# Seven half products for eight: the expanding products of two feed-forwards as 2x2 block products

## The chip, the core and the metric

The kernel runs on one core of a Trainium2 chip. The metric is the device time of one execution in microseconds (us). The engines named below are TensorE (PE, its weight loads as PEld), VectorE (DVE), ScalarE (ACT), GpSimd (POOL) and the queue of SyncE (SP) that issues the loads of the weights.

## What is computed

Two transformer-like blocks in float32 over 512 tokens of 1024 features, one after the other. Only the two feed-forwards matter here; D_FF is 4096 and D_FF_2 is 2816.

```python
# first block
hf = rmsnorm(x, norm_ff_g)
z = relu(hf @ w_ff1)                      # 1024 -> 4096: the expanding product
x = x + (z * z) @ w_ff2                   # 4096 -> 1024: the contracting product
# second block
h2 = modulate(rms_norm(x, g_norm2), shift2, scale2)
u = causal_depthwise_conv(h2 @ w_up, w_conv, b_conv)   # 1024 -> 2 * 2816, three taps along the tokens
val, gte = split(u, 2)
x = x + (1 + gate2) * ((val * silu(gte)) @ w_down)     # 2816 -> 1024
```

The modulation (shift, scale and gate) is silu(c) @ w_ada + b_ada and needs nothing of the first block.

## The kernel before

Features lie on partitions, tokens along the free axis. Every float32 operand of a product is kept as two float32r parts, a high part and the rest (low part), and every product is three matmuls: high x high, high x low, low x high (L242 to L244). One output tile is 128 features by 512 tokens: 8 contraction tiles x 3 matmuls of 512 columns, summed in one PSUM bank.

The weights come as pieces of 128 x 1024 (all contraction tiles of one output tile side by side). `Stream` (L63) loads them on SP's queue in the order of their use, lets ACT copy the high part (`_high`, L108) and DVE subtract it for the low part (`_low`, L116), and hands them out with `next` (L147). It works ahead by up to four split pieces (`ahead_split`, L130) and four loads, as far as slots of the pool are left: all activations, weight pieces and larger temporaries share 42 equal slots of 4 KB per partition. The pieces of w_ada stand between the weights (L1422): each is one multiply-and-sum on DVE (`ada_piece`, L401).

The order of work on each engine is written out by hand: instructions run on their engine in program order. Steps that wait for something are put off by "ticks" (`at`, L183, and `tick`, L187), and ticks are called after a product and in its middle.

The first block's output projection (L683 to L696) adds each output tile to x (L686), scales it by a gain into a split activation (L690, L691) and sums the squares, ACT's square (L321) added by POOL (L323). Then come four groups of 8 expanding tiles (L721: relu on ACT at L724, times itself on DVE at L725 with the product read from PSUM, split by `split_act`, L226 and L227) and 8 contracting tiles (L741, added by L734 and L737).

The second feed-forward (`ffn2`, L1278) begins with four half-token products (`proj_halves`, L1302), as its input is normalised by halves of the tokens (`norm2`, L1257, and `scaled`, L368). Then come groups of 8, 8 and 6 pairs of tiles (gate and value): each tile passes the convolution (`conv`, L1263: ACT's first tap from PSUM at L1266, two scalar-tensor-tensor steps of DVE that read PSUM at L1271), then silu (L1287), the product of value and gate (L1290) and the split. 8 contracting tiles follow each group.

Of the kernel before, what the change touches and what calls it, by code (L numbers as in the profile page):

```python
# [15 lines left out]
T = 512  # L16
# [3 lines left out]
SLOTS = 42  # L20
# [9 lines left out]
# Columns of the packed per-feature vectors: name -> number of 128-feature columns.  # L30
# [13 lines left out]
class Slots:  # L44
    """Equal slots of a pool, each a tag of its own; the one that was given back first is taken first."""
# [16 lines left out]

class Stream:  # L63
    """Weight pieces in the order of their use: DMA, split into two float32r parts, hand out.

    Pieces are loaded and split ahead of their use as far as slots are left."""

    def __init__(self, k, items, ahead_dma=4, ahead_split=4, reserve=5):
        self.k = k
        self.items = items  # L70
        self.ahead_dma = ahead_dma
        self.ahead_split = ahead_split
        self.reserve = reserve
        self.raw = {}
        self.half = []
        self.parts = {}
        self.n_dma = 0
        self.n_split = 0
        self.pos = 0

    def _dma(self, cuts=1):
        kind, ap, info = self.items[self.n_dma]
        n = ap.shape[-1]
        t = self.k.slots.take([128, n], F32, "raw")
        for i in range(0, n, n // cuts):
            self.k.nc.sync.dma_start(out=t[:, i:i + n // cuts], in_=ap[:, i:i + n // cuts])
        self.raw[self.n_dma] = t
        self.n_dma += 1

    def _high(self, cuts=1):  # L90
        """The next piece's high part, and what stands before the piece in the stream."""
        while True:
            i = self.n_split
            kind, ap, info = self.items[i]
            while self.n_dma <= i:
                self._dma()
            raw = self.raw.pop(i)
            k = self.k
            self.n_split += 1
            if kind == "w":  # L100
                break
            k.ada_piece(raw, info)
            k.slots.give(raw)
        n = ap.shape[-1]
        hi = k.slots.take([128, n], F32R, "hi")
        lo = k.slots.take([128, n], F32R, "lo")
        for j in range(0, n, n // cuts):
            k.nc.scalar.activation(out=hi[:, j:j + n // cuts], in_=raw[:, j:j + n // cuts], func=AF.Copy)  # L108
        self.half.append((i, raw, hi, lo))

    def _low(self, cuts=1):
        i, raw, hi, lo = self.half.pop(0)
        n = raw.shape[-1]
        for j in range(0, n, n // cuts):
            c = slice(j, j + n // cuts)
            self.k.nc.vector.tensor_tensor(out=lo[:, c], in0=raw[:, c], in1=hi[:, c].bitcast(F32), op=ALU.subtract)  # L116
        if self.items[i][2] == "turns":
            turns = lambda t: t.rearrange("p (k two c) -> p k two c", two=2, c=16)[:, :, 1, :]
            self.k.nc.vector.tensor_copy(out=turns(hi), in_=turns(lo).bitcast(F32))
        self.parts[i] = (hi, lo)  # L120
        self.k.slots.give(raw)

    def load_ahead(self, n=None):
        while (
            self.n_dma < min(self.n_split + (n or self.ahead_dma), len(self.items))
            and len(self.k.slots.avail) > self.reserve
        ):
            self._dma()

    def work_ahead(self):  # L130
        """A low part follows its high part by a piece, so that it doesn't wait for it."""
        while len(self.parts) < self.ahead_split:
            if self.n_split < len(self.items) and len(self.k.slots.avail) >= self.reserve + 2:
# [4 lines left out]
            else:  # L138
                if self.half and self.n_split == len(self.items):
                    self._low()  # L140
# [6 lines left out]
    def next(self):  # L147
        i = self.pos
        while self.items[i][0] != "w":
            i += 1  # L150
        while i not in self.parts:
            if not self.half:
                self._high()
            self._low()
        self.pos = i + 1
        w = self.parts.pop(i)
# [3 lines left out]

    def done(self, w):
        self.k.slots.give(*w)
# [3 lines left out]
class Kern:  # L166
    def __init__(self, ctx, tc, d, out):
# [6 lines left out]
        self.tp = P("tp", 8)  # L174
        self.sp = P("sp", 2)
        self.slots = Slots(P("slots", 1), "s", SLOTS)
        self.banks = Slots(P("ps", 1, space=bass.MemoryType.PSUM), "b", 8)
        self.now = 0
# [27 lines left out]
    def tmp(self, n=T):  # L206
        t = self.tp.tile([128, T], F32, tag="tmp", name="tmp")
        return t if n == T else t[:, 0:n]

# [8 lines left out]

    def v(self, name, k):
# [3 lines left out]
    def split_act(self, src, dst, t=slice(0, T)):  # L223
        """dst (hi, lo) <- src; src is float32 in SBUF or PSUM."""
# [6 lines left out]
    def gemm(self, acts, ps, w, t=slice(0, T), ks=None, first=True, last=True):  # L231
        """ps <- the weight tile's 128 columns times the activations, for the tokens t."""
        nc = self.nc
        hi, lo = w
# [43 lines left out]

    def proj_n(self, acts, ncol, consume):
        """Tokens on partitions, 512 columns at a time; two blocks of 128 tokens, then the others."""  # L280
        nc = self.nc
        for c in range(ncol):
            W = []
            for hf in range(2):
                banks = [self.bank() for _ in range(2)]
                for kp in range(4):
                    if hf == 0:
                        W.append(self.stream.next())
                    hi, lo = W[kp]
# [1245 lines left out]
```

## Time and profile before

| | |
|---|---|
| median of 3 runs | 1429.97 us (1429.94 to 1430.62) |
| span of the profiled execution | 1429.8 us |
| instructions | 17141 |
| PE busy | 1417.9 us, 99% |
| DVE busy | 814.6 us, 57% |
| ACT busy | 551.6 us, 39% |
| POOL busy | 104.5 us, 7% |
| PE's share of the chain that ended last | 96% |
| mean granted clock of PE | 0.995 |

A busy share is the time in which an engine had an instruction under way, over the span. Matmuls are pipelined and their ends are modelled, so what a matmul costs is read from the distance between two starts. The chain that ended last is followed back from the last instruction through whatever released each step.

### The profile page before, as it was taken

To read this page: it belongs to the slowest core of one execution; us is meant where nothing else is said; L and a number is where in the kernel's file an instruction comes from. 1 tells how busy PE (TensorE), PEld (TensorE's weight loads), DVE (VectorE), ACT (ScalarE), POOL (GpSimd) and SP (SyncE) were. 2 spreads that over 40 slices of the span, in tenths; PEclk is the share of its full clock that TensorE was granted. 3 is DMA by queue.
4 is the path that set the end of the run, shared out by engine and by line. 5 is a ranking of instruction groups with operands and counts; after the bars stand their busy time and mean duration, and the time that the engine had idled before them with its cause. 6 is when DMAs were issued, how large, how long until landed. Compare 5 with 4: busy or idle time off the path is not lost.

```text
span 1429.8 us, 17141 instructions
## 1 busy us (share of the span) xinstructions
PE 1417.9 (99%) x6918; PEld 1182.5 (83%) x6918; DVE 814.6 (57%) x1149; ACT 551.6 (39%) x860; POOL 104.5 (7%) x116
## 2 busy tenths in 40 slices
PE   9999999999999999999999999999999999999997
PEld 7888888888888888888889977777898888888887
DVE  6654355554457555554446748677666644653553
ACT  7533222222234423324134536556544422441433
POOL 1100000000002000000003360011210000000003
PEclk9999999999999999999999999999999999999999
DMA  8414444334364344442323210112322233233201
GB/s 299 140 56 147 148 164 160 115 123 131 124 230 133 131 143 154 134 161 80 116 84 106 75 58 30 59 60 74 133 89 89 89 103 118 83 93 94 73 12 60
DMA packets 46478, 159.73 MB, mean 112 GB/s; under 512 B 5152, under 2 KB 7328, under 8 KB 46400
## 3 DMA queue, kind: packets, MB, share of 16 engines
q1 hardware_dynamic: 45776, 156.94, 32.9%
q0 software_dynamic: 480, 1.70, 0.4%
q8 instruction: 54, 0.88, 0.2%
q14 instruction: 24, 0.20, 0.0%
q10 hardware_dynamic: 144, 0.00, 0.0%
HBM read 156.54 MB, written 2.10 MB: 111 GB/s over the span
## 4 chain that ended last, share of the span: by engine, by line
PE 96%; DVE 2%; ACT 1%; issue 0%; DMA 0%; DVEq 0%; POOLq 0%; POOL 0%; ACTq 0%
PE mm L242 28%; PE mm L244 28%; PE mm L243 28%; PE mm L297 2%; PE mm L298 2%; PE mm L299 2%; PE mm L895 1%; PE mm L833 1%; PE mm L832 1%; PE mm L591 0%; PE mm L355 0%; PE mm L879 0%; DVE cum L854 0%; DVE lo L116 0%; PE mm L1081 0%
## 5 line engine op out<-in xcount | busy, mean ns | idle before, releaser
L242 PE MATMUL mm<-act,hi 128*128 128x512 f32 (+1 forms) x1972 | 737.7, 374 | 0.0
L244 PE MATMUL mm<-act,lo 128*128 128x512 f32 (+1 forms) x1972 | 733.6, 372 | 0.0
L243 PE MATMUL mm<-act,hi 128*128 128x512 f32 (+1 forms) x1972 | 733.5, 372 | 0.0
L242 PEld LDWEIGHTS mm<-act,hi 128*128 128x128 f32 x1972 | 372.2, 189 | 65.9 <-issue 0.7
L244 PEld LDWEIGHTS mm<-act,lo 128*128 128x128 f32 x1972 | 372.1, 189 | 64.7
L243 PEld LDWEIGHTS mm<-act,hi 128*128 128x128 f32 x1972 | 372.3, 189 | 63.5
L116 DVE TENSOR_TENSOR lo<-raw,hi 128x1024 fp32r<-128x1024 f32 (+2 forms) x246 | 301.1, 1232 | 10.3 <-ACT hi L108 10.1
L108 ACT ACTIVATE hi<-raw 128x1024 fp32r<-128x1024 f32 (+2 forms) x246 | 250.7, 1038 | 99.4 <-DVE mod L401 41.8
L226 ACT ACTIVATE act<-tmp 128x512 fp32r<-128x512 f32 x86 | 54.3, 632 | 215.1 <-DVE tmp L662 73.1
L323 POOL TENSOR_TENSOR acc<-acc,tmp 128x256 f32<-128x256 f32 (+1 forms) x45 | 45.2, 1013 | 1100.5 <-ACT tmp L321 1100.4
L1271 DVE SCALAR_TENSOR_TENSOR tmp<-mm,vec,tmp 128x511 f32<-128x511 f32 x88 | 65.9, 749 | 81.5 <-ACT tmp L1266 79.9
L227 DVE TENSOR_TENSOR act<-tmp,act 128x512 fp32r<-128x512 f32 x86 | 59.5, 692 | 62.5 <-ACT act L226 62.5
L1266 ACT ACTIVATE tmp<-mm,vec 128x512 f32<-128x512 f32 x44 | 34.2, 777 | 83.5 <-PE mm L244 83.5
L724 ACT ACTIVATE tmp<-mm 128x512 f32<-128x512 f32 x32 | 19.1, 598 | 120.3 <-PE mm L244 120.3
L401 DVE CUSTOM_DVE_ANT_0 junk<-raw,csilu 128x1024 f32<-128x1024 f32 x48 | 63.0, 1312 | 0.0
L734 DVE TENSOR_TENSOR tmp<-mm,r 128x512 f32<-128x512 f32 (+1 forms) x38 | 23.0, 605 | 64.1 <-PE mm L244 64.1
L725 DVE TENSOR_TENSOR tmp<-tmp,mm 128x512 f32<-128x512 f32 x32 | 22.0, 688 | 64.6 <-ACT tmp L724 64.6
L1297 DVE SCALAR_TENSOR_TENSOR x<-mm,mod,x 128x512 f32<-128x512 f32 (+1 forms) x30 | 19.2, 644 | 67.2 <-PE mm L244 67.2
L297 PE MATMUL mm<-hi,act 128*128 128x512 f32 x128 | 52.2, 408 | 0.4 <-ACT hi L108 0.4
L298 PE MATMUL mm<-lo,act 128*128 128x512 f32 x128 | 50.9, 397 | 0.0
L299 PE MATMUL mm<-hi,act 128*128 128x512 f32 x128 | 50.6, 396 | 0.0
L321 ACT ACTIVATE tmp<-x 128x256 f32<-128x256 f32 (+1 forms) x58 | 24.9, 449 | 48.5 <-DVE x L1235 19.0
(180 smaller groups left out, 800.6 us busy)
## 6 DMA issues: line engine op xcount, KB each, us to landing
raw<-in_w_in_dram SPq DMA_DIRECT2D x65, 512.0 KB, 4.2
raw<-in_w_ff_dram SPq DMA_DIRECT2D x64, 512.0 KB, 3.7
raw<-in_w_ada_dram SPq DMA_DIRECT2D x48, 512.0 KB, 3.6
raw<-in_w_up_dram SPq DMA_DIRECT2D x44, 512.0 KB, 3.6
raw<-in_w_out_dram SPq DMA_DIRECT2D x16, 512.0 KB, 3.6
raw<-in_w_down_dram SPq DMA_DIRECT2D x16, 512.0 KB, 3.6
raw<-in_w_proj_a_dram SPq DMA_DIRECT2D x8, 512.0 KB, 3.5
raw<-in_w_proj_b_dram SPq DMA_DIRECT2D x8, 512.0 KB, 3.5
```

The lines of the kernel that those rows point to most:

```text
L108: k.nc.scalar.activation(out=hi[:, j:j + n // cuts], in_=raw[:, j:j + n // cuts], func=AF.Copy)
L116: self.k.nc.vector.tensor_tensor(out=lo[:, c], in0=raw[:, c], in1=hi[:, c].bitcast(F32), op=ALU.subtract)
L226: nc.scalar.activation(out=dst[:, 0, t], in_=src, func=AF.Copy)
L227: nc.vector.tensor_tensor(out=dst[:, 1, t], in0=src, in1=dst[:, 0, t].bitcast(F32), op=ALU.subtract)
L242: nc.tensor.matmul(out=ps, lhsT=hi[:, c], rhs=a[:, 0, t], start=st, stop=False)
L243: nc.tensor.matmul(out=ps, lhsT=hi[:, c], rhs=a[:, 1, t], start=False, stop=False)
L244: nc.tensor.matmul(out=ps, lhsT=lo[:, c], rhs=a[:, 0, t], start=False, stop=en)
L297: nc.tensor.matmul(out=b, lhsT=a[:, 0, t], rhs=hi[:, cs], start=(k == 0), stop=False)
L298: nc.tensor.matmul(out=b, lhsT=a[:, 0, t], rhs=lo[:, cs], start=False, stop=False)
L299: nc.tensor.matmul(out=b, lhsT=a[:, 1, t], rhs=hi[:, cs], start=False, stop=(k == KT - 1))
L401: nc.vector.tensor_tensor_reduce(out=junk, in0=raw, in1=self.csilu, op0=ALU.mult, op1=ALU.add, scale=1.0, scalar=0.0, accum_out=self.mod[: ...
L1271: nc.vector.scalar_tensor_tensor(out=y[:, n:T], in0=ps[:, 0:T - n], scalar=self.v("w_conv_2", j * 44 + i), in1=y[:, n:T], op0=ALU.mult, op ...
```

## The change

A pair of output tiles becomes a **unit**. Its weights are a 2x2 matrix of blocks (output tile x half of the 1024 contraction features), its input a 2x2 matrix (half of the features x half of the 512 tokens). Instead of the eight block products, seven are made, by sums and differences of blocks on both sides. A product is 4 contraction tiles x 3 matmuls of 256 columns.

- Weights: each unit loads two pieces of 1024 columns as before. POOL adds the block sums (one addition of 1024 columns, two of 512), and four `STEPS` are split: two of the loaded blocks, one loaded block alone (512 columns), and two pieces of sums.
- Input: DVE forms four combinations of 256 columns per pair of feature tiles, ACT and DVE split them (`combine` in the first block, during the output projection, whose tiles now run in the order 0, 4, 1, 5, ...; `combine_biased` in the second, during its first four half-token products). For this ACT writes gx, the gained x, once more, and the second block keeps its normalised input (`kept`).
- Output: three PSUM banks per unit instead of one per tile; ACT copies partial sums to SBUF between products (q1, q6, q5, q3), DVE adds (q2, q5, q4) into y0 and y1 in SBUF. What follows (relu and square as one scalar-tensor-tensor with max or min, or the convolution) now reads SBUF instead of PSUM. The second tile comes out negated: the convolution takes negated weights (`minus_w`).
- Order: products of two neighbouring units alternate; at the end of a group of the first feed-forward, the first contracting product begins early (`early`). The first two pairs of the second feed-forward stay as they were.
- The pieces of w_ada move: none between units; from piece 61 on, one behind every piece (before: behind every second one).
- 43 slots instead of 42, ten temporaries instead of eight, six of 256 columns for the copies; room for slots that are needed later is set aside (`promise`). The scratch of POOL's own DMAs shrinks (`dynamic_dma_scratch_size=2048`).

```diff
+PRODUCTS = {
+    "q1": ("w1", "b11"), "q2": ("w2", "b21"), "q3": ("w3", "b22"), "q4": ("w4", "t4"),
+    "q5": ("w5", "t1"), "q6": ("w6", "t2"), "q7": ("w7", "t3"),
+}
 class Stream:
+    STEPS = ("raw", "a2", "more", "sums")
+    PLACE = {"w1": (0, 0), "w4": (0, 1), "w2": (1, 0), "w6": (2, 0), "w3": (2, 1), "w7": (3, 0), "w5": (3, 1)}
...
+    def _sums(self, i):
...
+        eng = k.nc.gpsimd
+        r0, r1 = self.raw[i, 0], self.raw[i, 1]
+        two = k.slots.take([128, 1024], F32, "sums")
+        eng.tensor_tensor(
+            out=two.rearrange("p (b c) -> p b c", b=2), in0=r0.rearrange("p (b c) -> p b c", b=2),
+            in1=r1[:, 0:512].unsqueeze(1).to_broadcast([128, 2, 512]), op=ALU.add,
+        )
+        more = k.slots.take([128, 1024], F32, "more")
+        eng.tensor_tensor(out=more[:, 0:512], in0=two[:, 512:1024], in1=r0[:, 0:512], op=ALU.add)
+        eng.tensor_tensor(out=more[:, 512:1024], in0=more[:, 0:512], in1=r1[:, 512:1024], op=ALU.add)
+        self.sums[i] = (more, two)
...
+    def combine(self, hj, hk):
...
+        tt(c(ta, 0), hj[0], hj[1], ALU.subtract)
+        tt(c(ta, 1), hk[1], hj[1], ALU.subtract)
+        tt(c(tb, 0), c(ta, 1), hj[0], ALU.add)
+        tt(c(tb, 1), hk[0], c(tb, 0), ALU.subtract)
+        return self.split_pairs(ta, tb)
...
+    def seven(self, B, n, consume, lead=False, filler=None):
...
+            bank = {"q1": "a", "q6": "a", "q5": "a", "q3": "a", "q2": "b", "q7": "c", "q4": "c"}[name]
+            start = name in ("q1", "q2", "q7")
...
+            for j in range(4):
+                c = slice(j * 128, (j + 1) * 128)
+                bh, bl = B[bn][j]
+                en = j == 3
+                nc.tensor.matmul(out=ps, lhsT=hi[:, c], rhs=bh, start=start and j == 0, stop=False, skip_group_check=True)
+                nc.tensor.matmul(out=ps, lhsT=hi[:, c], rhs=bl, start=False, stop=False, skip_group_check=True)
+                nc.tensor.matmul(out=ps, lhsT=lo[:, c], rhs=bh, start=False, stop=en, skip_group_check=True)
...
+            if name in ("q1", "q6", "q5"):
+                e = U[name] = self.ev()
+                nc.scalar.activation(out=e, in_=ps, func=AF.Copy)
+            if name == "q2":
+                add(y0[:, f], U["q1"], ps)
+                self.pf(U["b"])
+            if name == "q5":
+                add(y1[:, l], U["q5"], U["c"][:, 0:HT])
+            if name == "q4":
+                add(y1[:, f], U["q6"], ps)
+                self.pf(U["c"])
+                consume(u, 1, y1)
+            if name == "q3":
+                nc.scalar.activation(out=y0[:, l], in_=ps, func=AF.Copy)
+                self.pf(U["a"])
+                consume(u, 0, y0)
...
+        while u < n:
+            run((u, "q1"), (u, "q2"))
+            run((u - 1, "q3"), (u, "q6"))
+            run((u - 1, "q4"), (u, "q7"), (u, "q5"))
+            u += 1
+        if filler:
+            filler()
+        run((n - 1, "q3"), (n - 1, "q4"))
...
+        for j in range(4):
+            self.at(5 + j, lambda j=j: TC.update({j: self.combine_biased(j)}))
         self.proj_halves(H, 4, lambda i, ps: up(i // 2, i % 2, ps), whole=True)
+        self.until(lambda: len(TC) == 4)
...
-        if i >= 22 and i % 2 == 0 and n < 48:
+        if i >= 22 and it[0] == "w" and n < 48 and (i % 2 == 0 or i > 60):
```

## Rows read from the trace of the kernel before

**Rows 1.** The page's busy time per engine, share of the span, instructions.

```profile
PE 1417.9 (99%) x6918; PEld 1182.5 (83%) x6918; DVE 814.6 (57%) x1149; ACT 551.6 (39%) x860; POOL 104.5 (7%) x116
```

**Rows 2.** Stretches: length, busy time and instructions per engine, granted clock, DMA share, GB/s.

```profile
409.00:452.50 43.50, 43.50 (x193) 36.05 (x192) 36.44 (x39) 19.91 (x26) 7.80 (x6) 1.00 0.61 217
452.50:496.00 43.50, 43.50 (x201) 36.26 (x200) 26.36 (x36) 17.47 (x24) 1.30 (x1) 1.00 0.40 132
496.00:539.60 43.60, 43.60 (x194) 36.12 (x193) 25.16 (x33) 10.56 (x11) 0.00 (x0) 1.00 0.44 147
1080.00:1145.00 65.00, 65.00 (x289) 53.81 (x288) 41.50 (x51) 28.91 (x38) 0.00 (x0) 1.00 0.27 83
...
1421.00:1429.00 8.00, 1.59 (x8) 1.20 (x8) 2.79 (x6) 0.46 (x1) 0.71 (x1) 0.62 0.35 131
```

**Rows 3.** PE's timeline (start, duration): 24 and 60 matmul distances, first and last.

```profile
480.01 0.39 PE L242 MATMUL mm<-act,hi 128*128 128x512 f32 x1
...
485.45 0.39 PE L242 MATMUL mm<-act,hi 128*128 128x512 f32 x1
...
1044.72 0.28 PE L244 MATMUL mm<-act,lo 128*128 128x256 f32 x1
...
1051.91 0.28 PE L244 MATMUL mm<-act,lo 128*128 128x256 f32 x1
```

**Rows 4.** DVE's groups by shape: count, busy us, mean ns, idle before.

```profile
L227 DVE TENSOR_TENSOR act<-tmp,act 128x512 fp32r<-128x512 f32 x86 | 59.5, 692 | 62.5 <-ACT act L226 62.5
...
L1271 DVE SCALAR_TENSOR_TENSOR tmp<-mm,vec,tmp 128x510 f32<-128x510 f32 x44 | 32.9, 749 | 1.6
```

**Rows 5.** ACT's groups by shape.

```profile
L108 ACT ACTIVATE hi<-raw 128x1024 fp32r<-128x1024 f32 x236 | 242.9, 1049 | 99.4 <-DVE mod L401 41.8 <-PE mm L243 30.7 <-PE mm L244 25.3
...
L1266 ACT ACTIVATE tmp<-mm,vec 128x512 f32<-128x512 f32 x44 | 34.2, 777 | 83.5 <-PE mm L244 83.5
...
L842 ACT ACTIVATE att<-mm 128x256 f32<-128x256 f32 x8 | 2.7, 386 | 0.6 <-PE mm L833 0.6
```

**Rows 6.** DVE's timeline in the second feed-forward's expanding products.

```profile
1105.67 0.69 DVE L227 TENSOR_TENSOR act<-tmp,act 128x512 fp32r<-128x512 f32 x1 [0.70 <-ACT act L226]
1106.28 1.22 DVE L116 TENSOR_TENSOR lo<-raw,hi 128x1024 fp32r<-128x1024 f32 x1
```

**Rows 7.** Timelines of POOL and DVE where they meet.

```profile
429.56 1.29 POOL L323 TENSOR_TENSOR acc<-acc,tmp 128x512 f32<-128x512 f32 x1 [4.31 <-ACT tmp L321]
...
429.60 2.33 DVE L116 TENSOR_TENSOR lo<-raw,hi 128x1024 fp32r<-128x1024 f32 x1
```

**Rows 8.** DVE's and POOL's groups by shape in 772 to 782.7 us alone.

```profile
L116 DVE TENSOR_TENSOR lo<-raw,hi 128x1024 fp32r<-128x1024 f32 x3 | 5.8, 1947 | 0.0
L737 DVE TENSOR_TENSOR x<-x,tmp 128x256 f32<-128x256 f32 x4 | 2.6, 650 | 0.1
L734 DVE TENSOR_TENSOR tmp<-mm,r 128x256 f32<-128x256 f32 x4 | 1.7, 417 | 0.5 <-PE mm L244 0.5
...
L323 POOL TENSOR_TENSOR acc<-acc,tmp 128x256 f32<-128x256 f32 x6 | 7.5, 1270 | 0.1
L323 POOL TENSOR_TENSOR acc<-acc,tmp 128x512 f32<-128x512 f32 x2 | 3.0, 1514 | 316.2 <-ACT tmp L321 316.2
```

**Rows 9.** POOL's timeline where DVE has no work with two SBUF inputs.

```profile
1398.32 0.74 POOL L323 TENSOR_TENSOR acc<-acc,tmp 128x256 f32<-128x256 f32 x1 [1.19 <-ACT tmp L321]
```

**Rows 10.** Timelines of DVE and PE at the second feed-forward's start.

```profile
1069.15 2.35 DVE L116 TENSOR_TENSOR lo<-raw,hi 128x1024 fp32r<-128x1024 f32 x2
1072.34 1.53 DVE L1271 SCALAR_TENSOR_TENSOR tmp<-mm,vec,tmp 128x511 f32<-128x511 f32 x2 [0.84 <-ACT tmp L1266]
...
1079.90 0.40 PE L242 MATMUL mm<-act,hi 128*128 128x512 f32 x1
```

**Rows 11.** DVE's timeline: x additions of the first block's output projection, first and last.

```profile
418.60 0.68 DVE L686 TENSOR_TENSOR x<-x,mm 128x512 f32<-128x512 f32 x1
...
452.49 0.69 DVE L686 TENSOR_TENSOR x<-x,mm 128x512 f32<-128x512 f32 x1 [0.57 <-PE mm L244]
```

More of the change, by code (lines that the diff above doesn't have):

```diff
@@ L90, in _high, with sums_ahead @@
+    def sums_ahead(self):
+        i = self.steps[self.n_split][0] if self.n_split < len(self.steps) else len(self.items)
+        for u in range(i, min(i + 3, len(self.items))):
+            if self.items[u][0] == "s" and u not in self.sums:
+                if (u, 1) in self.raw and self.room() >= self.reserve + 2:
+                    self._sums(u)
+                return
     def _high(self, cuts=1):
+        k = self.k
         while True:
-            i = self.n_split
+            n = self.n_split
+            i, j = self.steps[n]
@@ L106, in _high @@
[L106 to L109, printed above, removed]
-    def _low(self, cuts=1):
[L112 to L117, printed above, removed]
+        if kind == "w":
+            src, give = self.raw.pop((i, 0)), None
+            give = [src]
+        else:
+            self._sums(i)
+            src = (self.raw[i, 0], self.raw[i, 1], *self.sums[i])[j]
+            give = [src]
+            if j == 1:
+                src = src[:, 512:1024]
+            if j == 3:
+                del self.raw[i, 0], self.raw[i, 1], self.sums[i]
@@ new lines, in _high @@
+        self.n_split += 1
+        n_cols = src.shape[-1]
+        if j == 1:
+            both = k.slots.take([128, 2, 512], F32R, "a2")
+            hi, lo = both[:, 0, :], both[:, 1, :]
+            own = [both]
+        else:
+            hi = k.slots.take([128, n_cols], F32R, "hi")
+            lo = k.slots.take([128, n_cols], F32R, "lo")
+            own = [hi, lo]
+        for c in range(0, n_cols, n_cols // cuts):
+            k.nc.scalar.activation(out=hi[:, c:c + n_cols // cuts], in_=src[:, c:c + n_cols // cuts], func=AF.Copy)
@@ L118, in _low @@
+        self.half.append((n, src, give, hi, lo, own))
+    def _low(self, cuts=1):
+        n, src, give, hi, lo, own = self.half.pop(0)
+        cols = src.shape[-1]
+        for j in range(0, cols, cols // cuts):
+            c = slice(j, j + cols // cuts)
+            self.k.nc.vector.tensor_tensor(out=lo[:, c], in0=src[:, c], in1=hi[:, c].bitcast(F32), op=ALU.subtract)
+        if self.items[self.steps[n][0]][2] == "turns":
             turns = lambda t: t.rearrange("p (k two c) -> p k two c", two=2, c=16)[:, :, 1, :]
@@ L145, in split_one, with _need @@
         self._low(cuts)
[L147 to L151, printed above, removed]
+    def _need(self, n):
+        while n not in self.parts:
             if not self.half:
@@ L159, in next, with next_unit, get, used @@
         return w
+    def next_unit(self):
+        i = self.pos
+        while self.items[i][0] == "a":
+            i += 1
+        assert self.items[i][0] == "s"
+        self.pos = i + 1
+        return {"item": i, "got": {}, "left": [2, 1, 2, 2]}
+    def get(self, unit, name):
+        j, half = self.PLACE[name]
+        if j not in unit["got"]:
+            n = self.first[unit["item"]] + j
+            self._need(n)
+            unit["got"][j] = self.parts.pop(n)
+            self.load_ahead()
+            self.work_ahead()
+        hi, lo, own = unit["got"][j]
+        c = slice(half * 512, half * 512 + 512)
+        return hi[:, c], lo[:, c]
+    def used(self, unit, name):
+        j, half = self.PLACE[name]
+        unit["left"][j] -= 1
+        if unit["left"][j] == 0:
+            self.k.slots.give(*unit["got"][j][2])
+            self.load_ahead()
     def done(self, w):
-        self.k.slots.give(*w)
+        self.k.slots.give(*w[2])
         self.load_ahead()
```

288 lines of the change are left out of this document (218 added, 70 removed).

## The prediction

> **What bounds the kernel now.** I read the page's busy line first: TensorE (PE) is busy for 99% of the span, VectorE (DVE) for 57%, ScalarE (ACT) for 39%, GpSimd (POOL) for 7% [rows 1]. The stretch table then says what that average hides [rows 2]. In an expanding stretch of the first feed-forward DVE is busy 26.4 of 43.5 us, in one of the second 41.5 of 65.0, and in the first block's output projection (409 to 452.5) already 36.4 of 43.5, with POOL at 7.8. PE sets the time, at full granted clock (1.00, that is 2.4 GHz), but the other engines have room only of about a third in the expanding stretches, and almost none just ahead of them.
>
> The price of a product is read from start-to-start distances, not from the modelled durations. Matmuls of 512 columns start 24 in 5.44 us, 0.2267 us each; those of 256 columns, of which the kernel already has many, 60 in 7.19 us, 0.1198 us each [rows 3]. Half the columns cost 53%, not 50%.
>
> **PE, part by part.** A unit is two output tiles. Before it takes 48 matmuls of 512 columns, 48 x 0.2267 = 10.88 us; after, 7 x 12 = 84 of 256 columns, 84 x 0.1198 = 10.06 us. 0.82 us saved, times 16 units of the first feed-forward and 20 of the second (f of 2 to 21): 13.1 + 16.4 = 29.5 us, 2.1% of the time. That is the whole gain, and only if nobody makes PE wait.
>
> **DVE per unit.** A unit's weights are split as seven half pieces where there were four: 3 low parts of 1024 columns and one of 512, instead of 2 of 1024. Back to back a 1024 follows after 1.13 us [rows 10], a 512 after 0.61 [rows 6], so 4.0 us for 2.3. New are three 256-column additions out of PSUM, 0.42 long [rows 8], about 0.34 each back to back: 1.0. First feed-forward: two squarings at the 0.75 of a scalar-tensor-tensor [rows 4] (0.67 back to back) and two low parts at 0.61 make 2.6, total 7.6 us. Second: four convolution steps at 0.75, a product 0.69 [rows 4] and a low part 0.61 make 4.3, total 9.3 us, against PE's 10.06. To this come waits in DVE's own order: each activation split holds DVE for 0.70 us until ACT has the high part [rows 6]; the convolution additionally waits for ACT's first step (0.78) behind a weight's high part (1.05) [rows 5]. Laid out by hand in program order I get 9.5 us per unit in the first (two waits of 0.70, 0.5 more) and 11.5 in the second (0.70, 0.8 and 0.6). So without POOL the first just stays under PE, and the second exceeds even the old 10.88. ACT needs 6 to 7.5 us per unit (3.5 x 1.05, four copies of some 0.39, its tile steps at 0.63 to 0.78 [rows 5]): not the bound by itself, but it alternates with DVE.
>
> **POOL per unit.** One addition of 1024 and two of 512. A lone 256 takes 0.74 us [rows 9], a 512 1.29 [rows 7], so 0.55 for 256 more; the 1024 is not in the trace, 1.29 + 2 x 0.55 = 2.4. Sum 5.0 us: half of POOL's time, and harmless if the engines were independent. They are not: a low part that began 0.04 us after POOL's addition took 2.33 us for its usual 1.22, so 1.11 of POOL's 1.29 were lost [rows 7]. Where both have a queue (772 to 782.7), three low parts took 1.95 each for 1.22 and four additions with both inputs in SBUF 0.65 for 0.42, while the four multiplications that read PSUM kept their 0.42: DVE lost 2.2 + 0.9 = 3.1 us, and POOL's six additions of 256 and two of 512, 7.0 us alone, took 10.5 [rows 8]. So a microsecond of POOL's additions costs DVE between 3.1/7.0 = 0.44 and 1.11/1.29 = 0.86 us. Low parts, squarings and, now that their source has moved from PSUM to SBUF, the convolution steps all have two SBUF inputs.
>
> The Trainium skill (SBUF — State Buffer, § Who interferes with whom) says that a DVE instruction with two SBUF inputs and a GpSimd instruction that reads SBUF exclude each other for the whole instruction. The trace agrees on the mechanism. Taken at its full 5.0 us per unit, with nothing of it falling into DVE's waits, it would give cycles of 14.5 and 16.5 us and about 1595 us in the end, the top of my range; my sum goes by the two row ratios.
>
> By the rows a unit's sums cost DVE 2.2 to 4.3 us. I take 2.8: nearer to the stretch where both queue, as here. The units then last 12.3 us (first) and 14.3 us (second). For the low end, port work alone is 6.6 + 5.0 = 11.6 and 8.3 + 5.0 = 13.3.
>
> **How late DVE reaches PE.** q3 adds onto the bank that ACT must have copied after q5. ACT's copy is queued behind the split of the previous unit's tile, which waits for DVE. From q4's end PE has q7, q5, q1, q2 (5.7 us) of cover; the chain add, square, split, high part, copy takes 3.4 in the first feed-forward (2.3 to spare), with the convolution 5.5 in the second (nothing to spare). So DVE's rate becomes PE's.
>
> **Sums by stage.** (1) First feed-forward: look-ahead covers the sums of about one unit per group (slots: of 43, activations, combinations and promised outputs hold 25). Three of four units run at 12.3: 3 x 2.24 = 6.7 over PE, less 2.7 that the filler products (12 x 0.2267) and the longer start of the contracting product absorb: 4.0 x 4 groups = +16, less 13.1: **+3 us**. (2) Second: 17 units at 14.3 and 3 at 11.5 = 277.6 for 217.6: **+60**. (3) Its three group ends have no filler: q3 follows q5 at once, about 3 us each: **+9**. (4) Start of the second feed-forward: PE leaves the first four products at 1079.9 [rows 10]. Now four combinations lie in DVE's order between the four convolutions: four steps of 256 at about 0.45, a low part 0.61, another 0.67, 3.2 us with a short wait. From 1072.3, 4 x (1.5 + 3.2) + 2 x 2.1 = 23 us, to 1095.3; the first unit's low part (1.2) is issued after them because the promised slots stop the look-ahead, so its q1 starts at 1096.5: **+16**. (5) Output projection of the first block: DVE worked from 418.6 on without reaching PE until 452.5 [rows 11], so all that is added is late: four combinations (3.1 each; the last isn't needed for q2), two more modulation pieces brought forward (2.4), the first unit's sums (2.8) = 14.5, less q1 of two units (2.9): **+12**. The other moved modulation pieces lie beside contracting products with slack (DVE 3.7 of 5.44 us each). Extra slots, the smaller DMA scratch and the load order I cost at nothing: weights arrive beside computing, at a DMA share of 0.61 at most in these stretches [rows 2]; a late load would cost its microseconds once.
>
> Total 3 + 60 + 9 + 16 + 12 = +100. The profiled execution has a span of 1429.8, 0.2 below the median of 1429.97: **1530 us**.
>
> **Rivals.** *A, the forecast:* DVE, held up by POOL's port use, sets the second feed-forward; 0.68. Its own bounds: with port work alone (13.3, six units ahead of time), 14 x 13.3 + 6 x 11.5 - 217.6 = +38, group ends 0, first -11, starts +8 and +5: 1470. With 4.3 per unit: 303 - 217.6 = +85, ends +15, first +21, starts +20 each: 1591. *B, POOL costs DVE nothing,* because its additions fall into DVE's waits: first -13, second 20 x 0.62 = +12, ends +9, starts +16 and +10: 1464. For it: DVE waits up to 2.1 us per unit; against: POOL's 5.0 is more than that. 0.12. *C, the other side:* look-ahead moves enough low parts and sums into the contracting stretches (DVE at 25 of 43.6 us there [rows 2]) that the expanding ones stay PE's: -29.5, with starts of about +5 in all: 1405. It decides from the point at which DVE's unit falls under 10.06; against it, look-ahead is four parts, one unit of eight. 0.07. *D, worse:* PE waits so much that its clock falls. In the last stretch, where it is busy 1.6 of 8 us, the granted clock is 0.62, between its two levels of 1.2 and 2.4 GHz [rows 2]. At the lower level a unit is 20 us: if a third of the second's units run so, 7 x 6 = +42: 1570 to 1620. 0.10. *E:* gain and starts cancel, 1430; 0.03.
>
> **Numbers.** A measurement here tells 0.2% (3 us) from no change. Faster is C and 0.01 for what lies under B, 0.08; same 0.03; slower 0.89. The range takes in A's bounds and D's lower half; 1468 lies just above B: 1468 to 1595.
>
> **What would show it.** In the expanding stretches after: PE busy clearly under 90%, DVE near 90% with POOL at a third or more; low parts of 2 us and longer where they meet a POOL addition; ACT's copies of the banks waited for by PE; PE starts 0.12 us apart within a product; long PE gaps near 455 and 1080. I would be wrong if low parts stay at 1.22 beside POOL, if units pass in 10.1 us, or if the gaps at the two starts are missing.

## The result and the profile after

The changed kernel takes **2133.8 us** (median of 4 runs, 2128.5 to 2137.4) against 1430.3 of the kernel before beside it: 1.492 times as long (95% interval 1.489 to 1.494). Slower was forecast, but the size was not: 1530 was predicted, with 1595 as the top of the range.

The page of the changed kernel begins with the busy time, share of the span (2130.3 us) and instructions of each engine, as [rows 1] did for the kernel before:

```profile
PE 1643.0 (77%) x8214; PEld 1414.3 (66%) x8214; DVE 1001.7 (47%) x1378; ACT 655.8 (31%) x1068; POOL 314.9 (15%) x225
```

Two things stand in this line. PE's idle time is now 2130.3 - 1643.0 = 487.3 us; it was 1429.8 - 1417.9 = 11.9 [rows 1]. That is 475 of the 700 us by which the span grew. The other 225 us are PE *busy*: its matmuls have fewer columns in sum and yet took longer. And no engine is full; VectorE (DVE), which was forecast as the bound, works less than half of the time.

The stretches (length, busy time and instructions of PE, PEld, DVE, ACT and POOL, granted clock, DMA share, GB/s), two in the first feed-forward's expanding products and two in the second's, answer to [rows 2]:

```profile
470.00:576.00 106.00, 65.09 (x322) 59.40 (x322) 38.90 (x49) 25.69 (x41) 13.47 (x7) 0.70 0.13 46
644.40:746.30 101.90, 66.16 (x313) 60.12 (x312) 33.53 (x40) 21.11 (x34) 11.56 (x6) 0.70 0.16 57
1440.00:1560.00 120.00, 64.06 (x303) 58.17 (x303) 39.77 (x50) 30.42 (x47) 10.68 (x6) 0.67 0.09 31
1660.00:1760.00 100.00, 54.39 (x260) 49.49 (x261) 32.71 (x40) 23.33 (x36) 16.19 (x10) 0.68 0.09 32
```

Everyone waits: in the last stretch PE is busy 54 of 100 us, DVE 33, ACT 23, POOL 16. In the second stretch 313 matmuls of units take 101.9 us, that is 27 us for the 84 of a unit, where the two tiles took 10.9 before. The granted clock is 0.67 to 0.70, that is between its two levels of 1.2 and 2.4 GHz; it was 1.00 [rows 2]. What PE waits for stands in its table of waits (waiter and line, whom it waited for: us in total, times, longest):

```profile
PE mm L471 <- DVE lo L189: 225.4, 96, 8.3
PE mm L469 <- ACT hi L181: 137.6, 47, 19.4
PE mm L366 <- DVE lo L189: 71.9, 26, 7.2
PE mm L469 <- ACT a L181: 18.8, 19, 1.0
PE mm L364 <- ACT hi L181: 12.6, 2, 10.5
PE mm L469 <- ACT ev L478: 3.8, 4, 2.4
```

L469 to L471 are the three matmuls of a unit's products, L364 to L366 those of the ordinary tiles. They wait for the *high* and the *low part of a weight* (hi L181, lo L189), and hardly at all for the copies out of PSUM (ev L478) that the forecast had named. How one such wait arises is seen in a unit of the first feed-forward. First come rows of PE (in brackets: how long PE was idle before, and who ended it), then rows of DVE and of ACT in the same time:

```profile
702.76 0.58 PE L469 MATMUL mm<-tc,hi 128*128 128x256 f32 x1 [2.81 <-ACT hi L181]
...
711.93 0.39 PE L469 MATMUL mm<-tc,hi 128*128 128x256 f32 x1 [2.85 <-ACT hi L181]
...
713.19 0.58 PE L471 MATMUL mm<-tc,lo 128*128 128x256 f32 x1 [0.76 <-DVE lo L189]
713.57 0.41 PE L469 MATMUL mm<-tc,hi 128*128 128x256 f32 x1
713.78 0.41 PE L470 MATMUL mm<-tc,hi 128*128 128x256 f32 x1
```

```profile
709.58 0.69 DVE L974 SCALAR_TENSOR_TENSOR tmp<-tmp 128x512 f32<-128x512 f32 x1
710.96 0.69 DVE L349 TENSOR_TENSOR act<-tmp,act 128x512 fp32r<-128x512 f32 x1 [0.69 <-ACT act L348]
711.91 1.23 DVE L189 TENSOR_TENSOR lo<-sums,hi 128x1024 fp32r<-128x1024 f32 x1 [0.25 <-ACT hi L181]
```

```profile
710.30 0.63 ACT L348 ACTIVATE act<-tmp 128x512 fp32r<-128x512 f32 x1 [3.36 <-DVE tmp L974]
710.84 1.04 ACT L181 ACTIVATE hi<-sums 128x1024 fp32r<-128x1024 f32 x1
717.42 0.38 ACT L478 ACTIVATE ev<-mm 128x256 f32<-128x256 f32 x1 [5.54 <-PE mm L471]
```

ACT idles 3.36 us, does a step of the previous tile, and only then the high part (1.04) for which PE stands: the weight is split when its product is next, behind whatever the tile before it still has to do. The low part follows at 711.91; POOL has no work in this time. And after such a gap PE's 256-column matmuls start 0.21 us apart (713.57, 713.78; the granted clock is 0.50, the lower level, from 713.6 to 715.8) where [rows 3] have 0.12.

By stages, from the last addition onto x of each (L929, L994, L1503, L1592; before 452.5 [rows 11], 807.5, 1056.2 and 1419.9), in us of length, with three experiments that follow (e1_room3, e5_room3_no_sums, e9_order_no_sums; the last has no sums either):

| stage | before | after | look-ahead freed | ... and no sums | ... and new order |
|---|---|---|---|---|---|
| to the end of the first output projection | 452.5 | 469.8 | 457.6 | 454.0 | 453.6 |
| first feed-forward | 355.0 | 643.6 | 379.6 | 360.0 | 359.6 |
| between | 248.7 | 250.0 | 249.9 | 248.6 | 247.1 |
| second feed-forward | 363.7 | 756.6 | 464.7 | 437.6 | 419.8 |
| end | 9.9 | 10.3 | 9.7 | 9.3 | 9.8 |

The loss lies in the two feed-forwards, 289 and 393 us, with 17 more ahead of them.

### The profile page after: what moved, and what is told of

It is laid out like the page before. It is cut to its first block, busy times and chain, and to the rows that moved or that the text cites. A ratio compares the mean times of both kernels' runs of the same rounds, so it can differ in the third digit from the quotient of the medians.

```text
span 2130.3 us, 20399 instructions
## 1 busy us (share of the span) xinstructions
PE 1643.0 (77%) x8214; PEld 1414.3 (66%) x8214; DVE 1001.7 (47%) x1378; ACT 655.8 (31%) x1068; POOL 314.9 (15%) x225
## 4 chain that ended last, share of the span: by engine, by line
PE 68%; DVE 19%; ACT 9%; issue 2%; DMA 0%; SPq 0%; DVEq 0%; POOLq 0%; POOL 0%; ACTq 0%
PE mm L366 13%; PE mm L364 12%; PE mm L365 12%; PE mm L471 10%; DVE lo L189 8%; PE mm L469 7%; PE mm L470 7%; DVE tmp L1566 3%; ACT hi L181 2%; ACT act L348 2%; ACT tmp L1563 2%; PE mm L534 1%; PE mm L535 1%; PE mm L536 1%; DVE act L349 1%
## 5 line engine op out<-in xcount | busy, mean ns | idle before, releaser
L366 PE MATMUL mm<-act,lo 128*128 128x512 f32 (+1 forms) x1396 | 524.3, 376 | 71.9 <-DVE lo L189 71.9
L364 PE MATMUL mm<-act,hi 128*128 128x512 f32 (+1 forms) x1396 | 524.7, 376 | 12.6 <-ACT hi L181 12.6
L365 PE MATMUL mm<-act,hi 128*128 128x512 f32 (+1 forms) x1396 | 519.8, 372 | 0.0
L471 PE MATMUL mm<-tc,lo 128*128 128x256 f32 x576 | 219.9, 382 | 175.1 <-DVE lo L189 175.0
L366 PEld LDWEIGHTS mm<-act,lo 128*128 128x128 f32 x1396 | 270.8, 194 | 126.5 <-DVE lo L189 82.6
L364 PEld LDWEIGHTS mm<-act,hi 128*128 128x128 f32 x1396 | 271.9, 195 | 57.8 <-ACT hi L181 13.0
L365 PEld LDWEIGHTS mm<-act,hi 128*128 128x128 f32 x1396 | 271.2, 194 | 43.1
L189 DVE TENSOR_TENSOR lo<-raw,hi 128x1024 fp32r<-128x1024 f32 (+2 forms) x210 | 279.6, 1346 | 23.5 <-ACT hi L181 23.4
L471 PEld LDWEIGHTS mm<-tc,lo 128*128 128x128 f32 x576 | 159.2, 276 | 190.2 <-DVE lo L189 190.2
L469 PE MATMUL mm<-tc,hi 128*128 128x256 f32 x576 | 213.0, 370 | 85.1 <-ACT hi L181 85.1
L181 ACT ACTIVATE hi<-raw 128x1024 fp32r<-128x1024 f32 (+2 forms) x210 | 212.0, 1036 | 129.3 <-DVE lo L189 52.4
L469 PEld LDWEIGHTS mm<-tc,hi 128*128 128x128 f32 x576 | 159.9, 278 | 90.7 <-ACT hi L181 90.7
L470 PE MATMUL mm<-tc,hi 128*128 128x256 f32 x576 | 208.5, 362 | 0.0
L478 ACT ACTIVATE ev<-mm 128x256 f32<-128x256 f32 x108 | 41.4, 384 | 455.2 <-PE mm L471 455.1
L470 PEld LDWEIGHTS mm<-tc,hi 128*128 128x128 f32 x576 | 158.9, 276 | 0.0
L469 PE MATMUL mm<-act,hi 128*128 128x256 f32 x288 | 100.6, 349 | 56.3 <-ACT hi L181 52.5
L471 PE MATMUL mm<-act,lo 128*128 128x256 f32 x288 | 102.9, 357 | 50.4 <-DVE lo L189 50.4
L469 PEld LDWEIGHTS mm<-act,hi 128*128 128x128 f32 x288 | 71.9, 250 | 62.6 <-ACT hi L181 57.6
```

What stands on the lines that cost most here:

```text
L181: k.nc.scalar.activation(out=hi[:, c:c + n_cols // cuts], in_=src[:, c:c + n_cols // cuts], func=AF.Copy)
L189: self.k.nc.vector.tensor_tensor(out=lo[:, c], in0=src[:, c], in1=hi[:, c].bitcast(F32), op=ALU.subtract)
L364: nc.tensor.matmul(out=ps, lhsT=hi[:, c], rhs=a[:, 0, t], start=st, stop=False)
L365: nc.tensor.matmul(out=ps, lhsT=hi[:, c], rhs=a[:, 1, t], start=False, stop=False)
L366: nc.tensor.matmul(out=ps, lhsT=lo[:, c], rhs=a[:, 0, t], start=False, stop=en)
L469: nc.tensor.matmul(out=ps, lhsT=hi[:, c], rhs=bh, start=start and j == 0, stop=False, skip_group_check=True)
```

## The experiments

The theory after this reading: the look-ahead on weights, that is the splitting of a piece into its high and low part before its product is next, has all but stopped. In `work_ahead` a part is split ahead only where 7 slots are free beyond the promised ones (`room() >= reserve + 2`), loads go on from 6 and POOL's sums from 7, and both come first. With activations, combinations and promised outputs holding slots, loads and sums take the room down to 5 or 6, and splits find 7 no more. Following the code's rule through its order of issue, 117 of the 144 pieces of units are then finished only when their product is next (27 ahead of time), and 23 of the 173 ordinary tiles. For 50 of the 117 the high part was issued earlier and only the low part is late. In the kernel before it is one piece of 245.

The rivals: POOL's additions hold up DVE, as forecast; or PE's clock, which falls in the gaps, is the loss itself.

**The look-ahead freed.**

```diff
-            if self.n_split < len(self.steps) and self.room() >= self.reserve + 2:
+            if self.n_split < len(self.steps) and self.room() >= 3:
```

> The changed kernel, with one number changed: pieces are split ahead while 3 slots are free instead of 7 (loads and sums ahead keep theirs). Theory S (slots): in the changed kernel the loads and sums that are fetched ahead take the slots, so the splits find fewer than 7 free and each weight piece is split only when its product is issued, behind the previous tile's square or convolution; PE then waits for a chain of ACT and DVE at every piece, and at the lower clock. Then nearly all pieces are ready here and the time falls from 2134 us by at least 500, to 1400 to 1600, with low parts no longer named as what PE waits for. Theory P (POOL's use of the port and DVE's load, the prediction's own): the sums and the low parts are the same in number, so the excess of about 700 us stays for the most part, above 1900. If S holds for the bulk and P for the rest, 1500 to 1560.

1562.3 us (1558.0 to 1564.4), ratio 1.091 (1.089 to 1.094). One threshold takes back 571 of the 703 us; by the code's order 143 of the 144 pieces are now split ahead. Its busy line, and PE's largest waits:

```profile
PE 1432.5 (92%) x8214; PEld 1252.7 (80%) x8214; DVE 1027.3 (66%) x1378; ACT 646.7 (41%) x1068; POOL 319.2 (20%) x225
```

```profile
PE mm L469 <- ACT ev L478: 74.5, 41, 4.0
PE mm L469 <- ACT hi L181: 16.9, 2, 16.1
PE mm L471 <- DVE lo L189: 12.8, 3, 10.5
PE mm L366 <- DVE lo L189: 8.0, 1, 8.0
```

PE's idle time fell from 487 to 1561.5 - 1432.5 = 129 us and its busy time by 210: gaps and slow clock left together. The largest waits are now those that the forecast had described, for ACT's copies of the banks.

**A threshold between the two.**

```diff
-            if self.n_split < len(self.steps) and self.room() >= self.reserve + 2:
+            if self.n_split < len(self.steps) and self.room() >= 5:
```

> The changed kernel with splits ahead from 5 free slots on (7 in the change, 3 in e1_room3). Counted in the order of issue, 27 of 144 pieces of units are split ahead at 7, 125 at 5, 143 at 3. If what is lost is by the piece that is split only when its product is next, the 571 us between 7 and 3 are 116 pieces at 4.9, and 19 on demand give 1562 + 19 x 4.9 = about 1655 (1620 to 1690). If it is another effect of the threshold (a late load, a shortage that stops DMA), it needn't follow the count: near 1562 or above 1750.

1633.3 us (1631.7 to 1634.9), ratio 1.141, 71 us more than with 3. By the code's order 18 more pieces of units are late, all in the first feed-forward and all but one by their low part alone; 62 of the 71 us lie there (441.5 for 379.6), 3.4 a piece. The other 9 lie between the feed-forwards and are not explained. From 3 to 7 it is 571 us for 116 pieces of units and 21 ordinary tiles, 4.2 each. The loss grows with the number of pieces that are late, at no fixed price.

**The same loss in the kernel before**, where nothing else is changed: no further part of a weight is split ahead in the expanding stretches. What was split before a stretch begins (up to four pieces) stays ready. The lines of the first feed-forward; the second has the same:

```diff
         for grp in range(4):
             Z = []
+            self.stream.ahead_split = 0
             for f in range(8):
...
+            self.stream.ahead_split = 4
```

> The kernel before, whole products and no block sums, with one thing taken away: in both feed-forwards' expanding stretches no piece is split ahead, only when its product is issued. Theory S: each of the 72 tiles then waits for square or convolution, split, high part and low part of some 4 us and runs at the lower clock for a part of it: 72 x 4 to 9 us, 1720 to 2080. Theory P: no POOL work is there and DVE has a third of its time free, so the time stays within 30 us of 1430.

1782.2 us (1780.7 to 1783.7), ratio 1.246 (1.243 to 1.249): +352 us, with no block products, no sums and no promised slots. By the code's order 44 of the 72 tiles now find nothing of their piece split, which are the 44 waits for a high part below, and 7 find the low part missing. That is 8.0 us for each of the 44 (6.9 for each of the 51). PE's waits, which the kernel before has none of in these products:

```profile
PE mm L242 <- ACT hi L108: 172.6, 44, 4.8
PE mm L244 <- DVE lo L116: 40.4, 21, 5.2
```

**No sums in the changed kernel.** POOL's three additions of a unit are replaced by memsets of the same two tiles, so the block sums of the weights are left out.

```diff
-        eng.tensor_tensor(
...
-        )
+        eng.memset(two, 0.0)
...
-        eng.tensor_tensor(out=more[:, 0:512], in0=two[:, 512:1024], in1=r0[:, 0:512], op=ALU.add)
-        eng.tensor_tensor(out=more[:, 512:1024], in0=more[:, 0:512], in1=r1[:, 512:1024], op=ALU.add)
+        eng.memset(more, 0.0)
```

> The changed kernel without POOL's additions of weights: POOL fills the two tiles of sums with zeros instead (products with them are wrong by that), slots, splits and products as they are. Theory P: low parts return to 1.22 us, the time falls by most of the 700 us, under 1700. Theory S: the chain from product to split to product is untouched; POOL's additions delayed some low parts only, so 2050 to 2130.

2102.6 us (2101.2 to 2104.0): only 31 us less. In the kernel as changed, POOL's sums are a side matter, since DVE waits more than half of the time anyway.

**Zeros for the clock.** 12 products of zeros ahead of the first use of each piece keep PE at work while it would wait.

```diff
+        def warm(n):
+            for _ in range(n):
+                nc.tensor.matmul(out=self.wbank, lhsT=self.wzero[:, 0:128], rhs=self.wzero, start=True, stop=True)
...
+            if self.stream.PLACE[wn][0] not in U["w"]["got"]:
+                warm(12)
```

> The changed kernel with 12 products of zeros (bf16, 512 columns, into a bank of their own) on PE ahead of the first use of each weight step, in the time in which it would wait for the split: 12 x 0.213 = 2.6 us of a wait of some 4 us at 2.4 GHz. Theory C (a good part of the excess, about 200 us, is PE's matmuls at the lower clock, 0.213 apart instead of 0.120 for 256 columns): the granted clock rises from 0.85 towards 0.95 or more and the time falls, to 1900 to 2050. Without C (the clock only fills time in which PE would wait for the split anyway): the time is the same or longer by what the zeros take, 2130 to 2250.

2108.6 us (2107.6 to 2109.7), 25 us less, though the mean granted clock rose from 0.85 to 0.95. The time lies in neither of the two expected ranges. PE's timeline shows why this decides less than it was meant to:

```profile
700.34 0.28 PE L476 MATMUL mm<-tc,hi 128*128 128x256 f32 x1
700.46 0.28 PE L477 MATMUL mm<-tc,lo 128*128 128x256 f32 x1
700.81 2.54 PE L456 MATMUL mm<-wzero 128*128 128x512 bf16 x11
703.00 0.47 PE L475 MATMUL mm<-act,hi 128*128 128x256 f32 x1
```

The products do come 0.12 apart again, but the zeros take 2.5 us ahead of a piece, some 360 us in 144 places, and where the piece is ready sooner they are themselves the delay. So the run shows that the clock is higher when zeros fill the gaps, and that holding it in this way gains next to nothing while the weights come late. What the slow clock alone cost of the 703 us (at most the 225 us of busy time, with the saving of 29.5 added, 255) it doesn't tell.

**What is left with the look-ahead freed (+132 us): POOL or the order?** First the additions are left out again, as above, now with the threshold of 3.

> The changed kernel with the look-ahead freed (splits ahead from 3 free slots on, as in e1_room3, 1562 us) and POOL's 36 x 3 additions of weights replaced by memsets of the same tiles, so the block sums are left out. Theory P (what is left of the loss, +132 us, is mostly POOL's additions slowing DVE's two-input operations, as the prediction had it with 2.8 us a unit): 36 x 2.8 = 100 us go, about 1462 (1440 to 1490). Rival Q (it is the order on ACT and DVE, waits for copies of banks, that costs; POOL falls into waits): not more than 30 us go, 1530 to 1562.

1508.6 us (1504.9 to 1513.0), ratio 1.053 (1.051 to 1.056): 54 us less than with the sums, between the two expectations. Its busy line:

```profile
PE 1419.0 (94%) x8214; PEld 1240.5 (82%) x8214; DVE 936.3 (62%) x1378; ACT 646.9 (43%) x1068; POOL 175.1 (12%) x189
```

DVE does the same 1378 instructions in 1027.3 - 936.3 = 91.0 us less. That is what POOL's additions cost DVE: 2.5 us a unit in the mean. The 54 us are some 60% of it. That the memsets also finish sooner than additions hardly matters: with the sums ACT waits for one of POOL's sums once, for 5.8 us. The rest of the loss, 79 us, is not POOL's. Rows of ACT and of PE from the second feed-forward show a part of it, without additions beside them:

```profile
1144.62 1.04 ACT L177 ACTIVATE hi<-more 128x1024 fp32r<-128x1024 f32 x1
1145.57 1.04 ACT L177 ACTIVATE hi<-sums 128x1024 fp32r<-128x1024 f32 x1
1146.51 0.36 ACT L474 ACTIVATE ev<-mm 128x256 f32<-128x256 f32 x1
```

```profile
1146.92 0.39 PE L465 MATMUL mm<-tc,hi 128*128 128x256 f32 x1 [1.98 <-ACT ev L474]
1160.62 0.39 PE L465 MATMUL mm<-tc,hi 128*128 128x256 f32 x1 [2.27 <-ACT ev L474]
```

PE needs the copy (ev) of a bank that it will add onto, and the copy is queued behind two high parts that nobody needs yet. Most units of the first two groups are 13.2 to 13.8 us long here, without POOL's additions; in the third group they pass in 10.9 to 11.5 after the first.

**Copies ahead of the splits.** The look-ahead is freed as before; a product's copy out of PSUM is issued ahead of the splits of later weights.

```diff
             unit["got"][j] = self.parts.pop(n)
             self.load_ahead()
-            self.work_ahead()
...
-                consume(u, 1, y1)
...
                 self.pf(U["a"])
+            self.stream.work_ahead()
+            if name == "q4":
+                consume(u, 1, y1)
+            if name == "q3":
                 consume(u, 0, y0)
```

> As e1_room3 (1562 us), with the splits ahead issued behind a product's copy out of PSUM and not ahead of its matmuls. In e1_room3 PE waits 74.5 us in 41 places for ACT's copy of the bank that q5 leaves, which stands on ACT's queue behind one or two high parts of 1.05 us. Theory Q (order on ACT): these waits mostly go and the time falls by 40 to 80 us, to 1480 to 1520. Theory P (DVE, held up by POOL, is behind in any order; ACT's copy is only the last of a chain that DVE sets): the waits turn into waits for low parts, 1545 to 1570.

1544.4 us (1541.6 to 1547.5), ratio 1.079 (1.077 to 1.081): 18 us less, which is just under the range of theory P and far from that of Q. PE still waits 61.0 us in 29 places for these copies, now behind a Silu or a split of the tile, which wait for DVE.

**All copies of a step first.** The steps of the tiles (`consume`) too are issued at the end of a step of two or three products, behind the splits ahead; once with POOL's additions and once with memsets in their place.

```diff
-                consume(u, 1, y1)
...
-                consume(u, 0, y0)
+            if name == "q4":
+                late.append((u, 1, y1))
+            if name == "q3":
+                late.append((u, 0, y0))
...
                 if 0 <= u < n:
                     product(u, name)
+            self.stream.work_ahead()
+            while late:
+                consume(*late.pop(0))
             self.tick()
```

> e1_room3 with the order of issue changed: inside a step of two or three products only the copies and additions out of PSUM stand behind each product; the splits ahead, and then the tile's further steps (convolution or squaring, split), are issued at the end of the step. Nothing is left out. So a copy that PE waits for stands no longer behind a Silu or a split that waits for DVE. Measured so far: e1_room3 1562, copies ahead of the splits alone 1544. Theory Q (order on ACT's queue carries most of what is left beside POOL): 1490 to 1525. Theory P (DVE is late by its amount of work, about 11.8 us a unit in the second feed-forward with POOL's share): 1530 to 1550, and PE's waits go over to low parts and additions on DVE.

> e8_order with POOL's additions of weights replaced by memsets of the same tiles (block sums left out). Without them DVE has about 9.3 us of work a unit in the second feed-forward, under PE's 10.06. Theory Q: units run near PE's 10.1 to 10.6 us, and what is left over the kernel before is the two starts (16 and 5 to 10 us) less PE's saving (up to 29): 1430 to 1465. Theory P': the alternation of ACT and DVE inside a unit is a chain longer than PE's 10 us in any order: 1480 to 1510, as without the new order (1508.6).

With the sums 1553.7 us (1552.5 to 1557.4), ratio 1.086; without them 1491.6 (1490.9 to 1492.4), ratio 1.043 (1.041 to 1.045). The first lies just above the range of theory P and far from that of Q, the second within that of P'. The order is worth 9 us with the sums and 17 without. The kernel with the sums shows both cases side by side, since POOL works on some units of the second feed-forward and not on others. PE's first wait in each of four units; then DVE's rows in the first and, below the dots, in the third of them; then POOL's in the first:

```profile
1167.95 0.39 PE L469 MATMUL mm<-tc,hi 128*128 128x256 f32 x1 [3.17 <-ACT ev L478]
1182.94 0.58 PE L469 MATMUL mm<-tc,hi 128*128 128x256 f32 x1 [3.16 <-ACT ev L478]
1197.02 0.39 PE L469 MATMUL mm<-tc,hi 128*128 128x256 f32 x1 [1.04 <-ACT ev L478]
1208.39 0.39 PE L469 MATMUL mm<-tc,hi 128*128 128x256 f32 x1 [1.04 <-ACT ev L478]
```

```profile
1168.59 3.10 DVE L189 TENSOR_TENSOR lo<-raw,hi 128x1024 fp32r<-128x1024 f32 x1
1171.61 0.68 DVE L189 TENSOR_TENSOR a<-raw,a 128x512 fp32r<-128x512 f32 x1
1172.21 2.31 DVE L189 TENSOR_TENSOR lo<-more,hi 128x1024 fp32r<-128x1024 f32 x1
1174.44 2.57 DVE L1571 SCALAR_TENSOR_TENSOR tmp<-tmp,vec 128x511 f32<-128x511 f32 x2
...
1197.67 1.22 DVE L189 TENSOR_TENSOR lo<-raw,hi 128x1024 fp32r<-128x1024 f32 x1
1198.81 0.68 DVE L189 TENSOR_TENSOR a<-raw,a 128x512 fp32r<-128x512 f32 x1
1199.41 1.22 DVE L189 TENSOR_TENSOR lo<-more,hi 128x1024 fp32r<-128x1024 f32 x1
1200.82 1.54 DVE L1571 SCALAR_TENSOR_TENSOR tmp<-tmp,vec 128x511 f32<-128x511 f32 x2 [0.20 <-ACT tmp L1568]
```

```profile
1168.02 2.59 POOL L127 TENSOR_TENSOR sums<-raw 128x1024 f32<-128x1024 f32 x1 [5.14 <-DMA raw<-in_w_up_dram]
1171.86 1.58 POOL L132 TENSOR_TENSOR more<-sums,raw 128x512 f32<-128x512 f32 x1 [1.25 <-DVE lo L189]
1173.52 2.16 POOL L133 TENSOR_TENSOR more<-more,raw 128x512 f32<-128x512 f32 x1
```

Beside POOL's 6.3 us, two low parts take 3.10 and 2.31 instead of 1.22, and a pair of convolution steps 2.57 instead of 1.54: 4.0 us more on DVE, and the unit lasts 1182.94 - 1167.95 = 15.0 us. The unit that begins at 1197.02 meets no addition and lasts 11.4. In the kernel with memsets PE's waits of the second feed-forward come 11.4 us apart in most units. So the order carries 9 to 18 us and POOL 54 to 62. What is left stands in that kernel without sums. PE's rows at the second feed-forward's start:

```profile
1074.49 0.58 PE L361 MATMUL mm<-act,lo 128*128 128x256 f32 x1 [7.38 <-DVE lo L185]
1109.76 0.58 PE L465 MATMUL mm<-act,hi 128*128 128x256 f32 x1 [16.11 <-ACT hi L177]
```

PE idles 53.1 us in this stage: these 23.5, 16.3 for copies (ev), 10.2 in three places for ACT's split of the last tile of a group, and 3.1 in others. Its matmuls start, in sum, 19.8 us later than at 0.120 and 0.227 apart, for the most part after gaps; and the seven products for eight save 16.4. Together that is the +56.

The first feed-forward of the same kernel shows the saving bare. In its third group PE runs four units and the 12 products of 512 columns that fill the group's end without a gap and at the full clock:

```profile
639.60:683.00 43.40, 43.40 (x349) 42.60 (x348) 31.21 (x42) 24.12 (x39) 1.85 (x2) 1.00 0.29 98
```

Less 2.7 for the fillers that is 10.2 us a unit, PE's pace; theory P' holds in the second feed-forward only.

No combination that was run beats the kernel before. The best measured stages with the sums are 457.5 for 452.5 us, 370.6 for 355.0 and 454.9 for 363.7; even without them each changed stage is longer than before. So neither feed-forward is worth changing alone in any order that was run.

## Why the prediction was wrong, and where it held

**The step that failed** is a half sentence in the sum of the first feed-forward: "look-ahead covers the sums of about one unit per group (slots: of 43, activations, combinations and promised outputs hold 25)", and again in rival C, "look-ahead is four parts". The slots were counted, but against the wrong question: whether they leave room for sums, not whether they leave the 7 free ones that a split ahead asks for, behind loads that go on at 6. With 25 of 43 held, a unit's two raw tiles, two sums and seven parts already compete for 18. "Extra slots ... I cost at nothing" is the same step: its reason, the DMA share, speaks of loads and not of splits. All later terms took it for granted that a weight is split before its product is next. The forecast had noticed the very effect at one place ("the promised slots stop the look-ahead", start of the second feed-forward) and not asked how long it lasts. It lasts through both feed-forwards (34 of the 36 units have a piece that is late), and costs 571 of the 604 us by which the forecast missed.

**The mechanism forecast is real in a kernel that keeps its look-ahead,** and its total is near: that kernel takes 1562, 32 above the forecast. In part this is luck, as the terms show:

- *Units of 84 matmuls, 10.06 us.* The distance of 0.12 holds at full clock, and without the sums the first feed-forward reaches it (10.2 us). With the sums no group does, and in the second the waits cost more than the saving in every run. The 29.5 us are in PE's rows and were never left over.
- *DVE's order without POOL, 11.5 us in the second.* In the mean 13.1 as the code orders it and 11.5 with all copies first (PE's unit matmuls of the three groups, first to last start: 262.6 and 230.1 us for 20 units). By hand I had let ACT's copies pass the high parts that stand ahead of them in its queue.
- *POOL's 5.0 us a unit:* 5.8 in the changed kernel (2.56, 1.64 and 1.60), since POOL is held up as well. *Its cost to DVE, 2.8:* 2.5 in the mean, 4.0 where the three additions meet a full queue; the bounds were 2.2 and 4.3. The mean is 91.0 us of DVE for 36 x 5.0 us of POOL alone, 0.51 us for each, near the lower of the two ratios of [rows 7] and [rows 8]. So the rule of the Trainium skill (SBUF — State Buffer, § Who interferes with whom) holds as a mechanism, and taken at its full length it would have given too much. What of the rest falls into DVE's waits, and what beside operations that read PSUM, no run divides.
- *The cycle of 14.3 us.* 14.5 in the mean with the look-ahead freed (290.7 us for 20 units), but as 13.1 and 1.4 for the sums where the forecast had 11.5 and 2.8: two errors that cancel. With all copies first it is 11.5 and 2.0.
- *Stages (1) and (5), +15:* +29.7 with the look-ahead freed (5.1 and 24.6), of which a wait of 10.5 us for the first unit's low part at 469.2 lies at the place named, and +306 in the changed kernel. *Stages (2) to (4), +85:* +101, and +393.
- *The start of the second feed-forward, +16:* the gap named is there (16.1 us with the look-ahead freed, 19.4 in the changed kernel), but 35 us ahead of it stands a second one of 8.0, in which the first products wait for a low part queued on DVE behind the modulation; in the kernel before PE has no wait there. I had not looked for it.

**The rivals.** D, the falling clock, came true and larger: not a third of the second's units but most of both, with PE's busy time up by 225 us. I had priced it as a misfortune beside DVE's delay; here it came with waits at nearly every piece. B (POOL costs nothing) holds nearly in the changed kernel, where leaving the sums out gains 31 us, by B's own reason on a scale that B didn't have: DVE idles more than half of the time. C, the other side, did not come. Even what stood against it, a look-ahead of four parts, was too much: 27 of 144 pieces were ready.

**What was to show it.** PE under 90% came true (53 to 65%), and the gaps at the two starts. Low parts of 2 us and longer beside POOL's additions did occur (36 that ran beside one for over 0.6 us have a mean of 2.09), but in the mean of all they are 1.30 to 1.37. DVE near 90% with POOL at a third did not come (33 to 37 and 9 to 16% of these stretches), nor waits for ACT's copies (3.8 us in all), nor starts 0.12 us apart. By these signs the forecast's cause was present and set little; a larger one stood before it.

## What to carry to other kernels

Where buffers come from one pool, a change that holds more of them for longer must be followed through every threshold that asks for free ones: whoever asks for the most (here the splits ahead, at 7) is starved first, and silently, by those that ask for less (loads, at 6) or come first (sums). Price the loss of look-ahead before anything else, by the chain that then lies open for each piece, here 3.4 to 8.0 us a late piece, many times the saving of 0.82 us a unit. And where an engine queues copies that the matrix engine waits for, look at what is issued ahead of them: operations for later that could as well come behind.

## What was not expected of the hardware

- Zeros written by POOL cost DVE nothing: in the freed kernel without sums, 17 low parts of 1024 columns ran beside a memset for more than 0.3 us and took 1.22 us at most; beside additions that read SBUF they go to 2.3 and 3.1.
- POOL suffers in turn: in the changed kernel its additions of 512 columns take 1.27 to 1.30 us where they meet no instruction of DVE (16 of 72); the means of all are 1.60 and 1.64, and single ones reach 2.37. The 1024, estimated at 2.4, takes 2.37 to 2.40 alone.
- The granted clock of PE followed its gaps: 0.67 in a stretch where PE is busy 64 of 120 us, 0.91 in the same stretch of time when zeros fill it to 95, and 1.00 in the expanding stretches of the kernel before [rows 2], where PE is never idle. At the lower level a 256-column matmul follows after 0.21 us for 0.12.
